# Out projection of a decoder layer as seven half-size products instead of eight, with the gate applied to the outputs

## The chip, the cores and the metric

The kernel runs on one core of one Trainium2 chip. The metric is device time in microseconds; a program on one core has one time per run, and the median of the runs is used. Engines: TensorE (PE) multiplies, VectorE (DVE) and ScalarE (ACT) work on tiles in SBUF and PSUM, GpSimd (POOL) on tiles in SBUF; SyncE (SP) and POOL issue DMAs.

## What is computed

One decoder layer on 512 tokens of width 1024 in float32, and a final norm. The part around the change:

```python
merged = sigmoid(ga) * (out_a @ w_branch_swa) + sigmoid(gd) * (out_d @ w_branch_diff)
x = x + gate1 * (merged @ w_out)                      # out projection
h2 = rmsnorm(x, norm2_g) * (1 + scale2) + shift2
a, g = split(h2 @ w_up, 2)                            # up projection, 2 x 2816 columns
a = causal depthwise conv of width 3 over a, + conv_b
x = x + gate2 * ((gelu(a) * g) @ w_down)              # down projection
return rmsnorm(x, final_g)
```

## The kernel before

Every large product is made of three float32r matmuls: a float32 tile is split into a high part (a cast, on ACT) and a low part (tile minus high part, on DVE), and high x high, high x low and low x high are added up in PSUM. "Cast" and "low" below are these two operations; the function `split` (L118) does both, `split_pair` (L110) also takes the buffers. Weights pass through four raw buffers and three pairs of split buffers (`WB = 3`).

The stages in order: adaLN modulation and input projection; the two attention mixers; gate "d" and the branch merge (L938 to L985, eight column tiles j, one gate product and one branch product each); the **out projection** (L1023 to L1066 and `out_step`, L1245); residual, square sums and norm, the transposes of the normalised tokens (`turn2`) and their modulation (`early`, `mod_one`); the **up projection** in 11 pairs J of column tiles; the down projection with the last residual and norm.

In the merge, tile j is made on DVE in `tdall` (three slots) and split to `mgh[j]`, `mgl[j]` (L970 to L972). The out projection takes the merged columns as the stationary side and rows of `w_out` as the moving side: for k = 0 to 7 a row block of 128x1024 is loaded by SP, multiplied by gate 1 on DVE (L1029) and split. For each of four token blocks t and two column halves three 128x512 matmuls are added into one of eight PSUM banks: 8 x 4 x 2 x 3 = 192. The last three k run token by token, so that tokens 0 and 1 are through early: their residual sum (`add_x`), square sum (`square2`), norm (`norm_a` to `norm_c`; the power -0.5 is made on POOL, L177) and transposes lie beside the matmuls of tokens 2 and 3.

The up projection multiplies, for each pair J, halves of the tokens and halves of the rows in seven products instead of eight: a slot of 24 matmuls of 128x256 each, named p1, m5, m6, p2, m7, p3, p4 (`mul_slot`, L1185). It needs sums of weight blocks (made by accumulating DMAs on POOL's queue, `load_raw`, or by `sum_w` on DVE) and sums of the modulated tokens (`t1n`, `b12`, `b21`, on DVE). What follows a slot (copies, sums, convolution, GELU) is in `behind` and `conv`. The down projection uses the same scheme.

What sets the order: up to the out projection TensorE's order is written out and a scheduler places the other engines' instructions; from the last three k of the out projection to the end of pair 1 of the up projection (`man`, from L1326) all engines run in the order written. Every engine works through its queue in order.

Of the kernel before, what the change touches and what calls it, by code (L numbers as in the profile page):

```python
# [8 lines left out]
F32 = mybir.dt.float32  # L9
F32R = mybir.dt.float32r  # L10
# [4 lines left out]
P = 128  # L15
# [40 lines left out]
def kernel(  # L56
# [877 lines left out]
    def gpart(i, shape, name, dt=F32):  # L934
        return bp.tile(shape, dt, tag=f"gT{i}", name=name)


    mg = [[bp.tile([P, 2, S], F32R, tag="gx", bufs=5, name=f"mg{i}{b}") for b in "hl"] for i in range(2)]  # L938
    mg += [[bp.tile([P, 2, S], F32R, tag="gx", bufs=5, name="mg2h"), bp.tile([P, 2, S], F32R, tag="y", name="mg2l")]]
    mg += [[bp.tile([P, 2, S], F32R, tag="fgb", name="mg3h"), gpart(5, [P, 2, S], "mg3l", F32R)]]  # L940
    mgh, mgl = ([mg[k // 2][b][:, k % 2] for k in range(KT)] for b in range(2))
# [51 lines left out]
    TAIL = 3  # L993
    xnp = [gpart(i, [P, 2, D], f"xn{i}") for i in range(2)]
    g1b = gpart(4, [P, D], "g1b")
    g1bias = xnp[0][:, 0]
    brow(g1b, mod_rows[0])
    brow(g1bias, b_ada[0, 2 * D : 3 * D])
    nc.vector.tensor_add(g1b, g1b, g1bias)
    nc.vector.tensor_scalar_mul(g1b, g1b, 0.5)  # L1000
# [25 lines left out]
    def load_rows(src, k, name, gate):  # L1026
        r = raw_tile([P, D], name)
        nc.sync.dma_start(r, src[k * P : (k + 1) * P, :])
        nc.vector.tensor_mul(r, r, gate)  # L1029
        return split_pair(r, [P, D], name)  # L1030

    def tok_proj(acc, lh, ll, wts, nk, done, half_done=None):
        def step(k, t, hfs=(0, 1)):
            wh, wl = wts[k]
            a = lh(k)[:, t * P : (t + 1) * P]
            b = ll(k)[:, t * P : (t + 1) * P]
            for hf in hfs:
                sl = slice(hf * S, (hf + 1) * S)
                nc.tensor.matmul(acc[t][hf], a, wh[:, sl], start=k == 0, stop=False)
                nc.tensor.matmul(acc[t][hf], a, wl[:, sl], start=False, stop=False)  # L1040
            for hf in hfs:
                sl = slice(hf * S, (hf + 1) * S)
                nc.tensor.matmul(acc[t][hf], b, wh[:, sl], start=False, stop=k == nk - 1)

        for k in range(nk - TAIL):
            for t in range(NT):
                step(k, t)
        for t in range(NT):
            for hfs in ((0,), (1,)) if t == NT - 1 else ((0, 1),):
                for k in range(nk - TAIL, nk):  # L1050
                    step(k, t, hfs)
                if half_done is not None:
                    half_done(t, hfs)
            done(t)


# [3 lines left out]
    oacc = eight("oc")  # L1060
# [4 lines left out]
    wo = [load_rows(wout, k, f"wo{k}", g1b) for k in range(KT)]  # L1065

    def add_and_stat(acc, dst, x, wpool, name):
        ss = []
        for hf in range(2):
            sl = slice(hf * S, (hf + 1) * S)  # L1070
            nc.vector.tensor_add(dst[:, sl], x[:, sl], acc[hf])
            sq = wpool.tile([P, S], F32, tag="sq2", bufs=1, name=f"sq{name}{hf}")
            s1 = wpool.tile([P, 1], F32, tag="ss2", bufs=8, name=f"ss{name}{hf}")
            nc.scalar.activation(sq, dst[:, sl], AF.Square, accum_out=s1)
            if hf == 0:
                nc.vector.tensor_scalar(s1, s1, 1.0 / D, EPS, ALU.mult, ALU.add)
            ss.append(s1)
        rs = wpool.tile([P, 1], F32, tag="rs2", bufs=4, name=f"rs{name}")
        rstd_m2(rs, ss[1], 1, D, wpool, plus=ss[0])
        return rs  # L1080

# [69 lines left out]
    for i, name in enumerate(("p1", "p2")):  # L1151
        first_low = prep(0, name, (early_w[i][:, 0], early_w[i][:, 1]))
        W[1, name] = early_w[2 + i][:, 0], early_w[2 + i][:, 1]
    m5w = gpart(4, [P, 2, 4, 256], "m5w", F32R)
    with tc.issue_after(splits[-3][0].ins), tc.issue_after(splits[-3][1].ins):
        prep(0, "m5", (m5w[:, 0], m5w[:, 1]))
    with tc.issue_after(first_low[1].ins):
        sum_w(0, "m6")
# [86 lines left out]
    def out_step(t, k, hfs=(0, 1)):  # L1245
        wh, wl = wo[k]
        a, b = (m[k][:, t * P : (t + 1) * P] for m in (mgh, mgl))
        for hf in hfs:
            sl = slice(hf * S, (hf + 1) * S)
            nc.tensor.matmul(oacc[t][hf], a, wh[:, sl], start=k == 0, stop=False)  # L1250
            nc.tensor.matmul(oacc[t][hf], a, wl[:, sl], start=False, stop=False)  # L1251
        for hf in hfs:
            sl = slice(hf * S, (hf + 1) * S)
            nc.tensor.matmul(oacc[t][hf], b, wh[:, sl], start=False, stop=k == KT - 1)  # L1254

    ssq, r2, xns = {}, {}, {}

    def add_x(t, hf):
        sl = slice(hf * S, (hf + 1) * S)
        nc.vector.tensor_add(x1[:, t, sl], x1[:, t, sl], oacc[t][hf])  # L1260
# [7 lines left out]
    def norm_a(t):  # L1268
        nc.vector.tensor_scalar(ssq[t, 0], ssq[t, 0], 1.0 / D, EPS, ALU.mult, ALU.add)
        r2[t] = rstd_start(ssq[t, 1], 1, D, bp, plus=ssq[t, 0])  # L1270

    def norm_b(t):
        rs = bp.tile([P, 1], F32, tag="rs2", bufs=4, name=f"rso{t}")
        rstd_end(rs, *r2[t], 1, bp)
        xns[t] = xnp[t // 2][:, t % 2]
        return rs
# [45 lines left out]
    for k in range(KT - TAIL):  # L1322
        for t in range(NT):
            out_step(t, k)
    last = range(KT - TAIL, KT)
# [4 lines left out]
    def hi_early(i):  # L1330
        nc.scalar.copy(W[1, f"p{i}"][0], R[1, f"a1{i}"])

    def lo_early(i, q):
        hi, lo = W[1, f"p{i}"]
        V.tensor_sub(lo[:, q], R[1, f"a1{i}"][:, q], hi[:, q].bitcast(F32))

    hi_early(1)
    lo_early(1, slice(0, 4))
    for k in last:
        out_step(0, k)  # L1340
    add_x(0, 0)
    add_x(0, 1)
    square2(0)
    norm_a(0)
    norm_c(0, norm_b(0))
    hi_early(2)
    for k in last:
        out_step(1, k)
    add_x(1, 0)
    add_x(1, 1)  # L1350
    square2(1)
    lo_early(2, q0)
    norm_a(1)
    lo_early(2, q1)
    norm_c(1, norm_b(1))
    for k in last:
        out_step(2, k)
    add_x(2, 0)
    add_x(2, 1)
    out_step(3, last[0], (0,))  # L1360
    tps = {g: turn2(0, g) for g in (0, 1)}
    for k in last[1:]:
        out_step(3, k, (0,))
    for k in last:
        out_step(3, k, (1,))
    square2(2, (0,))
    early(0, "act")
    square2(2, (1,))
# [3 lines left out]
    early(1, "act")  # L1372
    early(1, "hi")
    norm_a(2)
    early(0, "lo")
    add_x(3, 0)
    early(1, "lo")
    square2(3, (0,))
    add_x(3, 1)
    square2(3, (1,))  # L1380
    for g in (2, 3):
        tps[g] = turn2(0, g)
    mul_slot(0, "p1")
    early(2, "vec")
    norm_a(3)
    early(3, "vec")
    for g in (2, 3):
        early(g, "act")
        early(g, "hi")
# [4 lines left out]
    mul_slot(1, "p1", (0,))  # L1394
# [18 lines left out]
    mul_slot(0, "p2", (0,))  # L1413
# [6 lines left out]
    mul_slot(0, "p2", (1,))  # L1420
    mul_slot(1, "p1", (1,))
# [10 lines left out]
    low_w(0, "m6")  # L1432
    lo_t(0, t1n, q0)
# [10 lines left out]
    sum_w(0, "p3")  # L1444
# [5 lines left out]
    V.tensor_sub(b12, b22, b12)  # L1450
    cast_w(0, "m7")
    hi_t(2, b12)
    V.scalar_tensor_tensor(b21, t1n, -1.0, b21, ALU.mult, ALU.subtract)
    hi_t(3, b21)
    behind(0, "m6")
    low_w(0, "m7")
    lo_t(2, b12)
    cast_w(1, "m5")
    mul_slot(0, "m7")
    lo_t(3, b21)  # L1460
    low_w(1, "m5")
    behind(0, "p3")
    mul_slot(1, "m5")
    behind(1, "p1")
    cast_w(0, "p4")
    sum_w(1, "m6")
# [3 lines left out]
    cast_w(1, "m6")  # L1470
    behind(0, "p2")
    conv_bias(0, 0)
    low_w(1, "m6")
    behind(1, "m5")
    mul_slot(1, "m6")
    sum_w(1, "p3")
# [388 lines left out]
```

## Time and profile before

| what | value |
|---|---|
| median of 3 runs | 696.21 us (696.03 to 697.71) |
| span of the profiled execution (it has no other time) | 696.6 us |
| out projection with its transposes | 314.66 to 360.96 us of the span |
| busy in 314.6 to 360.0: PE, DVE, ACT, POOL | 45.0, 26.6, 17.2, 3.8 us of 45.4 |
| busy in 374.0 to 412.0: PE, DVE, ACT, POOL | 38.0, 37.8, 26.1, 5.1 us of 38.0 |
| granted TensorE clock | 0.999 of full |

Times in the profile count from the start of the span. A group's row gives line, engine, operation, output<-inputs, shape, count, busy time, mean length in ns and idle time ahead of it. A timeline row gives start, length, engine, line, operation. A row of the chain that ended last gives start, length and what held the chain. Consecutive matmuls overlap, so their rate is read from starts, not lengths.

### The profile page before, as it was taken

The numbers are of one execution on the slowest core, as the hardware profiler recorded it, in microseconds if no ns is written. First come the engines' busy times: TensorE is split into PE (matmuls) and PEld (weight loads), VectorE is DVE, ScalarE is ACT, GpSimd is POOL, SyncE is SP. The second block draws the span as 40 slices with busy tenths as digits, with TensorE's granted clock in tenths as the row PEclk, the third lists the DMA queues.
The fourth block names the chain that finished last, engine by engine and source line by source line (L and its number), as shares of the span: only waits on it lengthen the run. The fifth ranks groups of instructions, "written<-read, shape, count | busy, mean of one in ns | idle before, by whom it ended". The sixth has DMA issues, their size and how long they took to land.

```text
span 696.6 us, 11353 instructions
## 1 busy us (share of the span) xinstructions
PE 685.0 (98%) x4247; PEld 598.4 (86%) x4247; DVE 573.3 (82%) x1093; ACT 377.9 (54%) x673; POOL 82.8 (12%) x100
## 2 busy tenths in 40 slices
PE   8999999999999999999999999999999999999995
PEld 8877877777787888888789999999999999888885
DVE  5999987888885557663679998888888999979997
ACT  5655675544552333331468756555555666655665
POOL 3000000000101000000020111111111102540300
PEclk9999999999999999999999999999999999999999
DMA  9985454454435676229817688786879738997903
GB/s 311 326 251 166 143 173 129 135 161 124 124 100 154 197 220 206 93 97 280 275 45 146 151 193 197 164 209 188 207 214 220 172 127 222 184 204 202 166 1 120
DMA packets 115862, 121.81 MB, mean 175 GB/s; under 512 B 4383, under 2 KB 93280, under 8 KB 115808
## 3 DMA queue, kind: packets, MB, share of 16 engines
q1 hardware_dynamic: 96894, 95.09, 43.0%
q0 software_dynamic: 18720, 25.73, 21.9%
q8 instruction: 33, 0.54, 0.3%
q10 hardware_dynamic: 194, 0.28, 0.1%
q14 instruction: 21, 0.17, 0.1%
HBM read 118.97 MB, written 2.11 MB: 174 GB/s over the span
## 4 chain that ended last, share of the span: by engine, by line
PE 64%; DMA 2%; DVE 1%; ACT 1%; issue 0%; POOLq 0%; DVEq 0%; ACTq 0%
PE up L1194 32%; PE dc L1809 15%; PE pgd L123 2%; PE pgd L125 2%; PE pgd L124 2%; DMA wo<-in_w_out_dram 2%; PE pB L125 1%; PE pB L123 1%; PE pB L124 1%; PE oc L1251 1%; PE oc L1254 1%; PE oc L1250 1%; PE pga L123 1%; PE pga L125 1%; PE pga L124 1%; DMA wa<-in_w_up_dram 1%
## 5 line engine op out<-in xcount | busy, mean ns | idle before, releaser
L1194 PE MATMUL up<-t,m_whi 128*128 128x256 f32 x512 | 93.1, 283 | 0.0
L1194 PEld LDWEIGHTS up<-t,m_whi 128*128 128x128 f32 x512 | 79.9, 192 | 0.0
L1194 PE MATMUL up<-t,m_wlo 128*128 128x256 f32 x256 | 72.5, 283 | 0.0
L1194 PE MATMUL up<-bh,p_whi 128*128 128x256 f32 x232 | 65.8, 283 | 0.0
L1194 PE MATMUL up<-bl,p_whi 128*128 128x256 f32 x232 | 65.7, 283 | 0.0
L1194 PE MATMUL up<-bh,p_wlo 128*128 128x256 f32 x232 | 65.7, 283 | 0.0
L810 DVE SCALAR_TENSOR_TENSOR arow<-ra,cs,arow 128x512 f32<-128x512 f32 x56 | 42.0, 750 | 23.1 <-DMA ra<-in_w_ada_dram 22.6
L1194 PEld LDWEIGHTS up<-t,m_wlo 128*128 128x128 f32 x256 | 49.2, 192 | 0.0
L1194 PEld LDWEIGHTS up<-bl,p_whi 128*128 128x128 f32 x232 | 44.6, 192 | 0.0
L1194 PEld LDWEIGHTS up<-bh,p_whi 128*128 128x128 f32 x232 | 44.6, 192 | 0.0
L1194 PEld LDWEIGHTS up<-bh,p_wlo 128*128 128x128 f32 x232 | 44.6, 192 | 0.0
L1103 POOL DMA_DIRECT2D s<-in_w_up_dram x21 | 27.0, 1360 | 141.0 <-DMA s<-in_w_up_dram 62.5
L1131 ACT CAST m_whi<-s 128x1024 fp32r<-128x1024 f32 x31 | 32.5, 1047 | 11.1 <-DVE s L1125 7.7
L1135 DVE TENSOR_TENSOR m_wlo<-s,m_whi 128x1024 fp32r<-128x1024 f32 x31 | 37.8, 1219 | 0.0
L1194 PE MATMUL up<-t,p_whi 128*128 128x256 f32 x176 | 32.2, 283 | 0.0
L177 POOL TENSOR_TENSOR r<-ms,mhalf 128x1 f32<-128x1 f32 (+1 forms) x16 | 13.1, 822 | 132.4 <-DVE ms L175 73.6
L829 POOL DMA_DIRECT2D mod_rows<-row x8 | 5.1, 642 | 194.2 <-ACT row L828 194.2
L724 ACT ACTIVATE sd<-sd,dmx 128x128 f32<-128x128 f32 (+3 forms) x32 | 17.7, 556 | 19.2 <-DVE dmx L716 19.2
L1194 PEld LDWEIGHTS up<-t,p_whi 128*128 128x128 f32 x176 | 27.5, 192 | 0.0
L1201 ACT ACTIVATE gT<-a,cv 128x512 f32<-128x512 f32 x22 | 17.7, 813 | 16.9 <-DVE a L1236 15.8
L1131 ACT CAST p_whi<-wa 128x1024 fp32r<-128x1024 f32 x18 | 18.7, 1041 | 12.6 <-PE up L1194 9.0
L1135 DVE TENSOR_TENSOR p_wlo<-wa,p_whi 128x1024 fp32r<-128x1024 f32 x18 | 22.0, 1223 | 3.8 <-ACT p_whi L1131 3.8
(479 smaller groups left out, 2085.7 us busy)
## 6 DMA issues: line engine op xcount, KB each, us to landing
ra<-in_w_ada_dram SPq DMA_DIRECT2D x32, 512.0 KB, 3.9
wa<-in_w_up_dram SPq DMA_DIRECT2D x22, 512.0 KB, 4.2
s<-in_w_up_dram SPq DMA_DIRECT2D x21, 512.0 KB, 4.8
s<-in_w_up_dram POOLq DMA_DIRECT2D x21, 512.0 KB, 6.4
adaw<-in_w_ada_dram SPq DMA_DIRECT2D x16, 512.0 KB, 5.3
w<-in_w_in_dram SPq DMA_DIRECT2D x12, 512.0 KB, 4.4
a<-in_w_up_dram SPq DMA_DIRECT2D x11, 512.0 KB, 4.7
b<-in_w_down_dram SPq DMA_DIRECT2D x10, 512.0 KB, 4.3
```

Of the source, the lines that this page charges most:

```text
L123: nc.tensor.matmul(o, lh, rh, start=start, stop=False)
L124: nc.tensor.matmul(o, lh, rl, start=False, stop=False)
L125: nc.tensor.matmul(o, ll, rh, start=False, stop=stop)
L177: nc.gpsimd.tensor_tensor(r0, ms, mhalf[:, :n], ALU.pow)
L724: exp = nc.scalar.activation(pm[m], pm[m], AF.Exp, bias=mx[:, m : m + 1], scale=slope, accum_out=lsum[:, m : m + 1])
L810: nc.vector.scalar_tensor_tensor(ac, r[:, a], cc, ac, ALU.mult, ALU.add)
L1103: nc.gpsimd.dma_start(dst, upblock(*blk), accum_op=ALU.add)
L1131: nc.scalar.copy(W[J, name][0], R[J, SRC[name]])
L1135: nc.vector.tensor_sub(lo, R[J, SRC[name]], hi.bitcast(F32))
L1194: nc.tensor.matmul(o[u], w[:, k, cu], b[:, k], start=name in ("p1", "m5", "p2") and k == 0 and x == 0, stop=k == 3 and x == 2, skip_group_ ...
L1201: nc.scalar.activation(grow(j), av[J][:, u], AF.Identity, bias=cv[:, 66 + j : 67 + j], scale=cv[:, 44 + j : 45 + j])
L1809: nc.tensor.matmul(bank2[u][:, sl], a[:, q, cu], b[:, q, sl], start=first_mm and x == 0, stop=last_mm and x == 2, skip_group_check=name no ...
```

## The change

The out projection is written as seven products of halves: tokens in halves (0 to 255, 256 to 511), inner rows as even and odd tiles of 128, columns in halves of 512. Each product is 4 inner tiles x 2 token blocks x 3 matmuls of 128x512. It needs sums of merged halves (`out_sums`: four sums of 128x256 per pair of column tiles on DVE, each split) and sums of blocks of `w_out`, made by accumulating DMAs on POOL's queue behind the low of the block's earlier form. Gate 1 no longer multiplies the weights; it multiplies the outputs (`post` on DVE, `minus_gated` on POOL, `gate_nlo`), and is itself loaded in two halves with its bias added by DMA. `norm_a` may take the halves' square sums in either order.

Then the hand-written order up to pair 1 is made anew: weights of p1, p2 and m5 of pair 0 are split within the out projection; p1 and p2 of pairs 0 and 1 run undivided; three lows of 128x1024 (p4's first, m5's and the second p2), the sums for m6 and p3 of both pairs and one sum of modulated tokens move to POOL. In all, POOL gets eight elementwise operations of 128x512 and eight of 128x1024; its queue gets eight loads of 512 KB from `w_out`, and SP's has six instead of eight. The tiles of `w_up` that follow take buffers which the out projection's merged tiles held.

```diff
-    mgh, mgl = ([mg[k // 2][b][:, k % 2] for k in range(KT)] for b in range(2))
+    SH = S // 2
+    NQ = KT // 2
+    od1 = [bp.tile([P, 2, S], F32R, tag="gx", bufs=5, name=f"od1_{q}") for q in range(NQ)]
+    ev = [bp.tile([P, NQ, SH], F32R, tag=g, name=f"ev{b}") for g, b in (("y", "h"), ("fgb", "l"))]
...
-            split(mgh[j], mgl[j], td)
+            q, odd = divmod(j, 2)
+            if odd:
+                split(od1[q][:, 0], od1[q][:, 1], td)
+                out_sums(q, tds[j - 1], td)
+            else:
+                split(ev[0][:, q], ev[1][:, q], td[:, :SH])
...
+    def out_sums(q, a, b):
+        lo, hi = slice(0, SH), slice(SH, S)
+        d, s2, s3, s4 = (sraw[:, i] for i in range(4))
+        nc.vector.tensor_sub(d, b[:, hi], a[:, hi])
+        nc.vector.scalar_tensor_tensor(s2, d, -1.0, a[:, lo], ALU.mult, ALU.subtract)
+        nc.vector.scalar_tensor_tensor(s4, s2, -1.0, b[:, lo], ALU.mult, ALU.subtract)
+        nc.vector.tensor_sub(s3, a[:, lo], a[:, hi])
+        for name, raw in (("d", d), ("s4", s4), ("s2", s2), ("s3", s3)):
+            split(sm[name][:, 0, q], sm[name][:, 1, q], raw)
...
-        nc.vector.tensor_mul(r, r, gate)
-        return split_pair(r, [P, D], name)
...
+    opass = dict(
+        m1=(oU, och, (0, 1)), p2=(oX, ostr, None), m5=(oV, och, (1, 1)), p3=(oV, osec, (0, 1)),
+        m6=(oU, och, (1, 0)), m7=(oU, osec, None), p4=(oU, och, None),
+    )
...
+    def oprep(name, g, on_pool=False):
+        _, src, add = opass[name]
+        wh = wp.tile([P, 2, S], F32R, tag="whi", bufs=WB, name=f"o{name}h{g}")
+        wl = wp.tile([P, 2, S], F32R, tag="wlo", bufs=WB, name=f"o{name}l{g}")
+        if on_pool:
+            nc.scalar.copy(wh, src[g])
+            nc.gpsimd.tensor_tensor(wl, src[g], wh.bitcast(F32), ALU.subtract)
+        else:
+            split(wh, wl, src[g])
+        if add is not None:
+            nc.gpsimd.dma_start(src[g], oblock(g, *add), accum_op=ALU.add)
+        ow[name, g] = wh, wl
...
+    def omul(name, gs=(0, 1), us=(0, 1)):
+        o = opass[name][0]
+        for g in gs:
+            wh, wl = ow[name, g]
+            for u in us:
+                for i in range(2):
+                    q = 2 * g + i
+                    ah, al = oside(name, q, u)
+                    for x, (a, b) in enumerate(((ah, wh), (ah, wl), (al, wh))):
+                        nc.tensor.matmul(
...
+    def post(u, acc, gate, add, first):
+        if first is not None:
+            V.tensor_add(acc[:, u], acc[:, u], first[u])
+        V.tensor_mul(acc[:, u], acc[:, u], gate)
+        d = x1h(u, add)
+        (V.tensor_sub if add else V.tensor_add)(d, d, acc[:, u])
...
+    def pool_gate(u, acc):
+        nc.gpsimd.tensor_tensor(acc[:, u], acc[:, u], g1b[1], ALU.mult)
+    def pool_sub(u, acc):
+        nc.gpsimd.tensor_tensor(x1h(2 + u, 1), x1h(2 + u, 1), acc[:, u], ALU.subtract)
+    def sum_pool(J, name):
+        src = R[J, SRC[name]]
+        nc.gpsimd.tensor_tensor(src, src, R[J, "a11" if name == "m6" else "a12"], ALU.add)
+    def lo_pool(J, name):
+        hi, lo = W[J, name]
+        nc.gpsimd.tensor_tensor(lo, R[J, SRC[name]], hi.bitcast(F32), ALU.subtract)
...
+    omul("m6")
+    V.tensor_add(ocv[:, 0], ocv[:, 0], oU[0])
+    oprep("m7", 1)
+    V.tensor_add(ocv[:, 1], ocv[:, 1], oU[1])
+    oprep("p4", 0, True)
+    hi_early(1, "p1")
+    post(0, ocv, g1b[1], 1, None)
+    square2(0, (1,))
+    post(1, ocv, g1b[1], 1, None)
+    oprep("p4", 1)
+    omul("m7")
+    square2(1, (1,))
+    nc.scalar.copy(ocv[:, 0], oU[0])
     norm_a(0)
+    nc.scalar.copy(ocv[:, 1], oU[1])
+    norm_a(1)
+    norm_halves(0, norm_b(0))
+    norm_halves(1, norm_b(1))
+    minus_gated(0, ocv)
+    minus_gated(1, ocv)
...
+    omul("p4", us=(0,))
     tps = {g: turn2(0, g) for g in (0, 1)}
+    omul("p4", us=(1,))
...
+    lo_pool(0, "m5")
     for g in (2, 3):
         tps[g] = turn2(0, g)
     mul_slot(0, "p1")
+    mul_slot(1, "p1")
...
     norm_halves(2, norm_b(2))
     norm_halves(3, norm_b(3))
     early(2, "lo")
     early(3, "lo")
-    mul_slot(1, "p1", (0,))
+    hi_early(1, "p2")
+    sum_pool(0, "m6")
+    lo_pool(1, "p2")
...
     low_w(0, "m6")
+    sum_pool(0, "p3")
...
     mul_slot(0, "m6")
-    sum_w(0, "p3")
     cast_w(0, "p3")
...
-    V.tensor_sub(b12, b22, b12)
+    nc.gpsimd.tensor_tensor(b12, b22, b12, ALU.subtract)
...
-    sum_w(1, "m6")
...
+    sum_pool(1, "m6")
...
+    sum_pool(1, "p3")
```

More of the change, by code (lines that the diff above doesn't have):

```diff
@@ L1059, with oblock @@
     braw = {}
-    oacc = eight("oc")
+    oU, oX, oV = (
+        [fbank("oc0"), fbank("oc1")], [sbank("oc2"), vbank("oc3")], [sbank("oc4"), sbank("oc5")],
+    )
+    wo4 = wout.rearrange("(q a p) n -> p q a n", a=2, p=P)
+    def oblock(g, a, hf):
+        return wo4[:, 2 * g : 2 * g + 2, a, hf * S : (hf + 1) * S]
+    ochain = gpart(4, [P, NQ, S], "ochain")
+    och = [ochain[:, 2 * g : 2 * g + 2] for g in range(2)]
+    for g in range(2):
+        nc.sync.dma_start(och[g], oblock(g, 0, 0))
@@ L1061 @@
+    for name, g in (("m1", 0), ("m1", 1), ("p2", 0)):
+        oprep(name, g)
     wa1 = gpart(2, [P, 2, 4, 256], "wa1")
@@ L1350, with hi_early @@
-    add_x(1, 1)
-    square2(1)
-    lo_early(2, q0)
-    norm_a(1)
[L1354 to L1360, printed above, removed]
-    tps = {g: turn2(0, g) for g in (0, 1)}
[L1362 to L1366, printed above, removed]
+    both = range(2)
+    def hi_early(J, name):
+        nc.scalar.copy(W[J, name][0], R[J, SRC[name]])
@@ L1383 @@
     mul_slot(0, "p1")
+    mul_slot(1, "p1")
+    add_nlo(1)
+    norm_a(2, 1)
+    early(2, "act")
+    square2(3, (0,))
     early(2, "vec")
-    norm_a(3)
+    early(3, "act")
+    norm_a(3, 1)
     early(3, "vec")
-    for g in (2, 3):
-        early(g, "act")
-        early(g, "hi")
+    early(2, "hi")
+    early(3, "hi")
     norm_halves(2, norm_b(2))
```

214 lines of the change are left out of this document (102 added, 112 removed).

## Prediction

> **What bounds the kernel now.** I read the head of the page first, then the chain that ended last, the waits of TensorE, and the busy time by stage.
>
> ```profile
> span 696.6 us, 11353 instructions
> PE 685.0 (98%) x4247; PEld 598.4 (86%) x4247; DVE 573.3 (82%) x1093; ACT 377.9 (54%) x673; POOL 82.8 (12%) x100
> ```
> ```profile
> PE pc L168 <- DMA crow<-in_c_dram: 2.4, 1, 2.4
> PE pga L123 <- ACT ta L840: 1.1, 1, 1.1
> PE oc L1251 <- DVE wo_l L120: 0.4, 1, 0.4
> PE td L742 <- DVE dls L727: 0.3, 1, 0.3
> PE pss L765 <- DVE qkv L465: 0.2, 1, 0.2
> ```
> ```profile
> 314.60:360.00 45.40, 45.02 (x202) 36.88 (x202) 26.58 (x44) 17.21 (x27) 3.82 (x4) 1.00 0.67 210
> 360.00:374.00 14.00, 14.00 (x121) 14.00 (x120) 12.80 (x27) 12.20 (x24) 4.49 (x4) 1.00 0.79 144
> 374.00:412.00 38.00, 38.00 (x319) 38.00 (x318) 37.79 (x53) 26.13 (x41) 5.11 (x4) 1.00 0.65 147
> ```
> In the stage rows the figures after the length are busy time of PE, weight loads, DVE, ACT and POOL, then granted clock, DMA share and GB/s. TensorE is busy 98% of the span and its five waits add up to 4.4 us. So a matmul that goes is time that goes, if nothing else comes late. The out projection (first row) has slack on DVE (26.6 of 45.4 us). The up projection behind it has none: DVE is busy 37.8 of 38.0 us, and TensorE doesn't wait. That is where this change can lose what it wins.
>
> **The change part by part.** *Matmuls.* Rates come from the chain in order of time (start, length):
>
> ```profile
> 314.66 0.43 PE oc L1250
> 347.75 0.45 PE oc L1254 x2
> 353.19 0.45 PE oc L1254 x2
> 360.09 0.88 PE th L1289 x8
> ```
> Between the second and third row stand four steps of six 128x512 matmuls: 24 in 5.44 us. Before, the stage runs 192 of them; after, 7 products x 4 row blocks x 2 token blocks x 3 = 168. The 24 that go are worth **-5.44 us**. From 314.66 to 360.09 are 45.43 us; 192 matmuls take 43.52 and the first eight transposes 0.88, so 1.03 us is waiting. The chain there runs through the last weight's DMA, cast and low; with the eight gated rows of w_out that wait goes: **-1.03 us**. What is late next is worked out below. A product now lasts 5.44 us; starting at 314.66 as before, p2, m5, p3, m6, m7 and p4 start at 320.1, 325.5, 331.0, 336.4, 341.9 and 347.3, and p4 with its transposes ends at 353.6.
>
> *Work ahead of the stage.* Each pair of merged column tiles gets four sums and four more lows of 128x256. From the rows below (0.42 us a 128x256, 0.69 a 128x512) a pair goes from 1.38 to 4.47 us on DVE, +12.4 us for four. Six of the eight gate products (1.22 us each) stood in this stage and go: net +5.1 us. ACT gets 16 more 128x256 casts. The stage is
>
> ```profile
> 262.00:314.40 52.40, 52.40 (x243) 42.32 (x241) 36.62 (x43) 17.21 (x24) 1.10 (x2) 1.00 0.41 133
> L1232 DVE TENSOR_TENSOR a<-a,up 128x256 f32<-128x256 f32 x4 | 1.5, 418 | 0.0
> L1260 DVE TENSOR_TENSOR x<-x,oc 128x512 f32<-128x512 f32 x8 | 5.2, 682 | 1.3 <-PE oc L1254 1.3
> L1135 DVE TENSOR_TENSOR m_wlo<-s,m_whi 128x1024 fp32r<-128x1024 f32 x7 | 8.5, 1220 | 0.0
> L1131 ACT CAST m_whi<-s 128x1024 fp32r<-128x1024 f32 x7 | 7.3, 1050 | 5.0 <-DVE s L1125 5.0
> ```
> DVE goes to about 42 of 52.4 us, beside gate matmuls: nothing on the path. Without that cover it would be 5 us. m1 needs only the even columns, ready one gate earlier; p2, the first to need the last odd column, has 5.4 us.
>
> *Weights.* Fourteen casts and lows replace eight: a product needs 2 x 1.05 us on ACT and 2 x 1.22 on DVE in 5.44 us. That fits. With three buffers a cast waits until the matmuls of the weight three places earlier are through, which is one product (5.44 us) ahead of its own use; cast and low one after the other take 2.27.
>
> *Accumulating loads.* The sums of w_out blocks are made by eight 512 KB loads on POOL's queue, each behind the low that still reads the old block, and behind the s1 load for the up projection, which waits there for its base.
>
> ```profile
> s<-in_w_up_dram POOLq DMA_DIRECT2D x21, 512.0 KB, 6.4
> ```
> ```profile
> s_t<-in_w_up_dram POOLq DMA_DIRECT2D x1, 512.0 KB, 12.2
> ```
> The median landing is 6.4 us over the run, 12.2 for the one issued in this stage. m5's first weight is split at 320.1 + 1.05 + 1.22 = 322.4; its block lands at 328.8 to 334.6, and m6's low is done at 331.1 to 336.9, needed at 336.4. That low can't be earlier than 333.3 (buffer free at 331.0). p4's block then lands at 339.7 to 349.1, and with cast and POOL's low (below) is ready at 341.8 to 352.0, needed at 347.3. So this chain costs 0 to 4.7 us. (On POOL the gate product of m5's result waits for ACT's copy, 0.9 us after 331.0, and p4's loads are queued behind it; they wait for m6's low longer than that.) SP's next w_up loads now wait for tiles that the product p4 still reads, so fewer transfers compete late in the stage; I stay near the lower end and take **+0.6 us**. Those delayed loads (s3 and s1 of the first pairs) go out at about 354 and are first needed at m7 of pair 0, near 377: covered by 23 us; with 12.2 us each and their second loads behind three POOL operations they would still land by then.
>
> *Outputs and norm.* Tokens 0 and 1 are complete after m6, at 341.9 (its first half 1.36 us earlier, at 340.5). Then on DVE in order: add 0.69, m7's low 1.22, add 0.69, four of 0.69, p4's low 1.22: 6.6 us. Rows of the norm follow: two pairs of small ones, two powers on POOL at 0.55, ends and halves (0.57 each), some 3 us. That ends at 350.1 from the earlier start and 351.5 from the later; the transposes between the halves of p4 want it at 350.0. So 0 to 1.5 us; I take **+0.7**. Queued behind it are the lows of the first modulated tiles, due 3.6 us later behind p4's second half.
>
> *POOL's arithmetic.* Eight 128x512 and eight 128x1024 operations with two inputs, of a kind that the trace doesn't have. Nearest rows:
>
> ```profile
> L153 POOL TENSOR_SCALAR_AFFINE_SELECT ddf<-ddf 128x512 f32<-128x512 f32 x1 | 0.6, 605 | 0.0
> L150 POOL TENSOR_SCALAR_AFFINE_SELECT dsw<-dsw 128x256 f32<-128x256 f32 x1 | 0.4, 391 | 0.0
> ```
> One input costs 0.214 us per 256 and 0.177 fixed. So 128x1024 takes 1.03 us if a second input is free, 1.89 if it is read after the first; 0.61 and 1.03 for 128x512. I take the upper, because nothing in the trace shows POOL reading two at once: 8 x 1.03 + 8 x 1.89 = 23.4 us on an engine busy 3.8 of 45.4 us. Its results are due late enough: p4's low is bounded above, after p4 come transposes (0.88) and p1 of both pairs (5.76), so the next transposes stand at 360.3, m6 of pair 0 at 370.8 and p3 at 373.6; their sums are due 2.3 us ahead, at 368.5 and 371.3. The Trainium skill, GPSIMD Engine Reference, section 3.1, measures 4497 ns for 2048 columns, an estimate of 2.25 us for 1024; by it POOL would have 27 us of work. No row here shows such an operation.
>
> *The up projection anew.* p1 and p2 of both pairs follow each other undivided; the matmuls are the same. The stretch from the transposes of tokens 2 and 3 to m5 shrinks:
>
> ```profile
> 365.27 0.87 PE th L1289 x8
> ```
> ```profile
> 374.02 3.04 PE L1194 MATMUL up<-t,m5w 128*128 128x256 f32 x24
> 376.90 0.40 PE L1194 MATMUL up<-t,m_whi 128*128 128x256 f32 x2
> ```
> It was 8.75 us and becomes two transposes of 0.88 and two products of 2.88: 7.5. DVE's lead there falls by 1.2 us. Four 128x1024 operations leave DVE in the dense stretch, 4 x 1.13 = 4.5 us by the spacing of
>
> ```profile
> 376.92 1.22 DVE L1450 TENSOR_TENSOR braw<-braw 128x1024 f32<-128x1024 f32 x1
> 378.05 1.22 DVE L1453 SCALAR_TENSOR_TENSOR braw<-s_t,braw 128x1024 f32<-128x1024 f32 x1
> 406.76 1.22 DVE L1135 TENSOR_TENSOR m_wlo<-s,m_whi 128x1024 fp32r<-128x1024 f32 x1
> 408.58 0.40 PE L1194 MATMUL up<-t,m_whi 128*128 128x256 f32 x2
> ```
> The last pair is where DVE's lead is least: the low ends at 407.98, its product starts at 408.58, 0.6 us. With 4.5 - 1.2 us more it is 3.9: no wait, if POOL leaves DVE alone. I cost it at **0**.
>
> **Sum.** 696.6 - 5.44 - 1.03 + 0.6 + 0.7 = 691.4 us of span. The profiled execution has no time beside its span; it lies 0.4 above the median 696.21 of the runs (696.03 to 697.71). So the forecast is **691.0 us**.
>
> **Rivals.** *POOL holds up DVE (slower).*
>
> ```profile
> 353.43 0.94 POOL L177 TENSOR_TENSOR r<-ms,mhalf 128x1 f32<-128x1 f32 x1 [3.67 <-DVE ms L175]
> 362.39 0.55 POOL L177 TENSOR_TENSOR r<-ms,mhalf 128x1 f32<-128x1 f32 x1 [2.55 <-DVE ms L175]
> ```
> ```profile
> 353.27 0.68 DVE L1335 TENSOR_TENSOR early<-wa,early 128x512 fp32r<-128x512 f32 x1
> 362.61 0.21 DVE L183 SCALAR_TENSOR_TENSOR rt<-r,ms 128x1 f32<-128x1 f32 x1
> ```
> The same power takes 0.55 us alone and 0.94 when it is issued while DVE reads two SBUF tiles: POOL waits for DVE. Whether DVE waits for POOL as long, no row tells; the small operation at 362.61 inside the power kept its usual 0.2 us, which speaks against. If it does: (a) p4's low on POOL, 1.89 us, stands before the norm, which has no slack; (b) behind the second power POOL has the sum for m6 and p2's low, 3.78 us, before DVE may end norm and lows of tokens 2 and 3. Behind the powers of tokens 0 and 1 (done at about 349.5) four gate operations (1.03 each), m5's low (1.89) and two powers end at 356.6, half a us later where the squares come last, ends and halves 1.5 later: 358.5, 1.8 ahead of 360.3. Costs 2.0; (c) the four moved operations hold DVE 7.6 us where they spared it 4.5; with the shorter lead 7.6 - 4.5 + 1.2 - 0.6 = 3.7 us. Together 7.6: **698.6 us**. It turns slower once POOL holds DVE for two thirds of that. The Trainium skill, SBUF — State Buffer, section "Who interferes with whom", has this rule: a VectorE instruction with two SBUF inputs and a GpSimd instruction that reads SBUF exclude each other, and whichever started first keeps the other out to its end. The trace agrees in one direction (0.94 against 0.55).
>
> *The sums of w_out land late.* The 4.7 us of that chain instead of 0.6: **695.1 us**. For it: 12.2 us in this stage, and a DMA share of 0.67 there with half a dozen more software loads; against it: SP's loads that wait.
>
> That the products aren't fewer is excluded: 168 matmuls are in the program's order.
>
> **How the numbers follow.** Forecast 0.50, POOL against DVE 0.28, late sums 0.14, other lateness of the seven products' preparation that costs more than the 6.5 us won 0.08. No new wait gives 696.2 - 6.5 = 689.7, the lower end; the upper reaches past the first rival to 699.5, leaving out part of it and the last case. A measurement here tells 0.3% (2.1 us) from no change: faster is the forecast and a third of the late sums, 0.54; same is the rest of these and the mild part of POOL's case, 0.16; slower 0.30.
>
> **What would show it.** After: 168 oc matmuls at 5.44 us a product; no TensorE wait over 1 us between m1 and m5 of pair 0; POOL's 128x1024 at 1 to 1.9 us while DVE's stay at 1.22. POOL's case shows as DVE groups grown beyond 1.22 and waits of up on lows; late sums as ACT casts of m6 or p4 waiting for ochain. I am wrong if the first matmul of m1 starts later than 314.7, or if a product waits for a buffer.

## The result, and the profile after

The changed kernel takes **717.04 us** (median of 4 runs, 715.9 to 718.14) against 696.23 beside it: ratio 1.0295, 95% interval 1.0278 to 1.0312. The forecast was 691.0 with a range to 699.5. The profiled execution took 717.19 us, with a span of 715.4.

The head of the page after, with the rows of busy tenths for TensorE, its granted clock and the DMAs, and the chain that ended last:

```profile
span 715.4 us, 11408 instructions
PE 688.2 (96%) x4223; PEld 599.0 (84%) x4223; DVE 597.8 (84%) x1122; ACT 393.7 (55%) x705; POOL 124.0 (17%) x126
PE   8999999999999999998876999999999999999995
PEclk9999999999999999999988999999999999999998
DMA  9976445444455664669737399878779738997902
PE 79%; DVE 11%; DMA 4%; issue 3%; ACT 1%; POOL 1%; SPq 0%; POOLq 0%; DVEq 0%; ACTq 0%
```

TensorE has 24 matmuls fewer (4223 for 4247), as the change says, yet it is busy 3 us longer, and in two slices in the middle its granted clock falls. In the slices around 330 to 390 us it isn't full any more. The waits of TensorE say for what:

```profile
PE up L1226 <- DVE t L1339: 4.3, 1, 4.3
PE th L1308 <- DVE xn L1301: 4.2, 3, 3.6
PE oc L1113 <- DVE om6l L120: 2.3, 1, 2.3
PE oc L1113 <- ACT oc_fgb L1365: 1.9, 1, 1.9
PE oc L1113 <- ACT oc_v L1428: 1.8, 1, 1.8
PE pB L125 <- DVE wbd L120: 1.3, 1, 1.3
```

The first five of these lie between the start of m1 (314.50) and the end of m5 of pair 0, the last in the merge. From m1 to p3 of pair 0 both kernels do the same products, but for the 24 matmuls, and this stretch holds most of the result. The busy time by stretch, before and after (columns: length, then busy time of PE, weight loads, DVE, ACT, POOL, granted clock, DMA share, GB/s):

```profile
314.66:379.79 65.13, 64.75 (x369) 56.61 (x370) 45.11 (x74) 33.68 (x57) 8.31 (x8) 1.00 0.67 186
```
```profile
314.50:397.93 83.43, 68.10 (x346) 57.99 (x346) 69.95 (x89) 45.62 (x78) 40.51 (x28) 0.90 0.73 177
330.00:350.00 20.00, 15.81 (x61) 12.08 (x61) 16.86 (x16) 11.33 (x17) 10.75 (x9) 0.91 1.10 227
```

It is 18.3 us longer (83.43 for 65.13), where the forecast had 5.2 less. Behind it the kernels run alike: 317.5 us remain after, 316.8 before. Ahead of it, in the merge, there is a smaller loss; the rows of 300 to 310 before and after, and what DVE stood still for:

```profile
300.00:310.00 10.00, 10.00 (x45) 8.26 (x44) 6.06 (x7) 4.38 (x6) 0.00 (x0) 1.00 0.30 105
```
```profile
300.00:310.00 10.00, 8.67 (x39) 6.85 (x38) 5.51 (x10) 3.28 (x6) 2.09 (x2) 1.00 0.51 84
304.98 0.43 DVE L1026 TENSOR_SCALAR g1b<-g1b 128x512 f32<-128x512 f32 x1 [4.39 <-DMA g1b<-in_b_ada_dram]
```

DVE waits 4.39 us for the second half of gate 1 with its bias, the low of a branch weight behind it comes late, and TensorE waits 1.3 us (`pB <- DVE wbd`). From the first branch product to the out projection are 57.5 us, 55.9 before.

In the stretch from m1 on DVE shows 69.95 us of busy time instead of 45.11, POOL 40.51 instead of 8.31, and in 330 to 350 the DMA engines are full (share 1.10) at only 227 GB/s. What DVE's busy time is made of shows in the timeline, on DVE and then on POOL (start, length):

```profile
373.57 2.43 DVE L183 SCALAR_TENSOR_TENSOR rt<-r,ms 128x1 f32<-128x1 f32 x1
376.64 0.21 DVE L183 SCALAR_TENSOR_TENSOR rt<-r,ms 128x1 f32<-128x1 f32 x1
383.45 6.86 DVE L1339 TENSOR_TENSOR t<-s_t,t 128x512 fp32r<-128x512 f32 x2
391.60 1.29 DVE L1339 TENSOR_TENSOR t<-s_t,t 128x512 fp32r<-128x512 f32 x2
```
```profile
373.58 2.41 POOL L1379 TENSOR_TENSOR s_t<-s_t,wa 128x1024 f32<-128x1024 f32 x1
383.61 3.85 POOL L1379 TENSOR_TENSOR s_t<-s_t,wa 128x1024 f32<-128x1024 f32 x1
386.35 3.40 POOL L1530 TENSOR_TENSOR braw<-braw 128x1024 f32<-128x1024 f32 x1
```

The first operation of DVE works on one column, usually takes 0.21 us, and lasts 2.43: until POOL's operation of 2.41 us, started beside it, is over (375.99 and 376.00). The two lows at 383.45 usually take 1.29 us together. They last 6.86, across two of POOL's operations that follow each other (the second ends at 389.75); this is the wait of 4.3 us inside m5. So two theories stand: **POOL's two-input operations keep DVE out** (the prediction's first rival, dearer than it was priced), and **blocks of w_out land late** (the second). A third is that DVE simply has too much to do, whoever works beside it; a fourth, that the falling clock costs the time.

### The profile page after: what moved, and what is told of

Its sections match the earlier page's. It is cut to its first block, busy times and chain, and to the rows that moved or that the text cites. A ratio compares the mean times of both kernels' runs of the same rounds, so it can differ in the third digit from the quotient of the medians.

```text
span 715.4 us, 11408 instructions
## 1 busy us (share of the span) xinstructions
PE 688.2 (96%) x4223; PEld 599.0 (84%) x4223; DVE 597.8 (84%) x1122; ACT 393.7 (55%) x705; POOL 124.0 (17%) x126
## 4 chain that ended last, share of the span: by engine, by line
PE 79%; DVE 11%; DMA 4%; issue 3%; ACT 1%; POOL 1%; SPq 0%; POOLq 0%; DVEq 0%; ACTq 0%
PE up L1226 30%; PE dc L1889 15%; PE a L360 4%; PE pga L123 2%; PE pga L125 2%; PE pga L124 2%; PE oc L1113 1%; DMA osec<-in_w_out_dram 1%; PE pgd L123 1%; PE pgd L124 1%; PE pgd L125 1%; PE pw L123 1%; PE pk L123 1%; DMA ra<-in_w_ada_dram 1%; PE pw L124 1%
```

## The experiments

Names for short: "all on DVE" is the changed kernel with POOL's sixteen operations on DVE; osec0 is the block of w_out for p3 and m7.

**POOL's operations given back to DVE, all and in part.**

```diff
-        nc.gpsimd.tensor_tensor(acc[:, u], acc[:, u], g1b[1], ALU.mult)
+        nc.vector.tensor_tensor(acc[:, u], acc[:, u], g1b[1], ALU.mult)
```
The same edit in all six places for the first run; in the four of the out projection and the early weights (eleven operations) for the second; in `sum_pool` and at `b12` (five operations) for the third. (The expectations speak of twelve operations, and of three or four sums; the edits move eleven, and four sums with one subtraction.)

> All sixteen of POOL's operations with two inputs go back to VectorE, at the same places in the order; nothing else changes. Theory 1 (a POOL operation that reads two SBUF tiles and a VectorE operation on SBUF tiles keep each other out, and TensorE's clock falls after the waits that follow): the waits at the transposes between the halves of p4 (4.4 us in the changed kernel), at m5 of pair 0 (6.2 with its slow matmuls) and the slow matmuls behind them go, 12 to 18 us of 717.0: 699 to 705 us, granted clock back over 0.9 in 355 to 395 us. Rival (VectorE has simply too much work in these stages, whoever else works): eight operations of 0.69 and eight of 1.13 us, 14.6 us of work, are put on top of it: 717 to 728 us.

> Only the twelve POOL operations of the out projection's stage and of the first up products (four gate products, four subtractions, the lows of p4, of m5 and of p2 on pair 1... those that belong to the outputs and to early weights) go back to VectorE; the three sums and the subtraction of the dense stretch stay on POOL. Theory 1: the wait at the transposes and the slow second half of p4 go, 6 to 10 us; the wait before m5 of pair 0 stays at 3 us or more: 707 to 711 us. Rival (too much work on VectorE): 717 to 723 us.

> Only the three or four sums for the up projection's weights and one subtraction of 128x1024 go back to VectorE; the out stage keeps its POOL operations. Theory 1: the wait inside m5 of pair 0 (4.6 us) with its slow matmuls (about 2.5 us) goes, the waits between p4's halves stay: 709 to 712 us. Rival (too much work on VectorE): 717 to 722 us.

Measured: **706.95** (706.61 to 707.74), 712.21 and 711.23 us. The parts give 4.8 and 5.8 us, together 10.6; all at once 10.1. That is below the range that the first theory gave the first two runs (12 to 18, 6 to 10), and clearly against the third theory: 14.6 us more work on DVE made the kernel faster. The long wait at m5 (`up <- t`) is gone in all three runs; in the second the stretch of m5 shrank to 4.4 us too, against its expectation. The wait at the transposes between p4's halves (`th <- xn`) is down to 0.4 us in the first and the second run and stays in the third. In the second the sum that POOL kept, 2.37 us from 369.94, holds DVE's `rt` of one column (2.38 from 369.95), and the next transposes wait 2.7 us for it:

```profile
PE oc L1113 <- ACT oc_fgb L1365: 2.5, 1, 2.5
PE oc L1113 <- ACT oc_v L1428: 2.5, 1, 2.5
PE up L1226 <- DVE t L1339: 1.0, 2, 0.6
```
```profile
PE oc L1113 <- ACT oc_fgb L1365: 4.5, 1, 4.5
PE th L1308 <- DVE rt L183: 2.7, 1, 2.7
```
```profile
PE th L1308 <- DVE xn L1301: 3.6, 1, 3.6
PE oc L1113 <- ACT oc_fgb L1365: 2.4, 1, 2.4
PE up L1226 <- DVE t L1339: 1.0, 2, 0.5
```
(All on DVE; the second run; the third.) With all on DVE 10.6 us over the kernel before remain, and the longest waits are now those of out products.

**The mechanism by itself**, in the kernel before, which has none of the change. Four operations of 128x1024 on POOL in the dense stretch, each reading something that DVE has just made, writing a tile that is free. One of the four in the first run is shown; the second run has `tensor_scalar` of `bl[:, 2]` (times 2, plus 1) in its place, the third the same on one column and then a `memset` of 128x1024.

```diff
     V.tensor_sub(bl[:, 2], b22, bh[:, 2].bitcast(F32))
+    nc.gpsimd.tensor_tensor(gT[5][:, 0:2].rearrange("p a s -> p (a s)"), x1[:, 0], bl[:, 2].rearrange("p a n -> p (a n)").bitcast(F32), ALU.mult)
     behind(0, "m5")
     low_w(0, "p3")
...
```

> The kernel before, with four more multiplications of 128x1024 on POOL in the dense stretch of the up projection; each reads two tiles of SBUF that are long done, and nothing reads what they write. Each starts when a VectorE low is done, apart from the others. Theory 1 (POOL and VectorE exclude each other): VectorE loses 2.4 us to each, 9.6 in all, less the 0.6 to 2 us that it is ahead there: 703 to 706 us. If a POOL operation leaves VectorE alone: 696 us, VectorE's 128x1024 operations at 1.22 us throughout.

> The kernel before with four more operations of 128x1024 on POOL at the same places as in the run that gave 703.69 us, but with one input (times two plus one) instead of two. If what excludes VectorE is that POOL reads SBUF at all: as long as POOL's operation lasts, about half of the 7.4 us or more: 699 to 704 us. If it takes two POOL inputs: 696 us.

> The kernel before with four fills of 128x1024 on POOL at the same places, each behind a 128x1 operation of POOL's that reads the low just made: POOL only writes. If POOL's reading is what excludes VectorE: 695.5 to 697 us, VectorE's 128x1024 operations at 1.22 us beside the fills. If any POOL work on SBUF does: 699 us or more.

Measured: **703.69** us with two inputs (+7.4, interval of the ratio 1.009 to 1.012), **698.57** with one (+2.0, 1.0019 to 1.0038; its range began at 699), **696.54** with fills (0.9986 to 1.0007: nothing). The first one's timeline, DVE and POOL:

```profile
371.11 1.22 DVE L1125 TENSOR_TENSOR s_t<-s_t,wa 128x1024 f32<-128x1024 f32 x1
372.25 3.43 DVE L1447 TENSOR_TENSOR bl<-braw,bh 128x1024 fp32r<-128x1024 f32 x1
375.60 1.21 DVE L1135 TENSOR_TENSOR p_wlo<-s_t,p_whi 128x1024 fp32r<-128x1024 f32 x1
376.73 3.42 DVE L1452 TENSOR_TENSOR braw<-braw 128x1024 f32<-128x1024 f32 x1
```
```profile
371.33 3.26 POOL L1443 TENSOR_TENSOR gT<-x,t 128x1024 f32<-128x1024 f32 x1 [6.23 <-DVE t L1320]
375.81 3.26 POOL L1448 TENSOR_TENSOR gT<-x,bl 128x1024 f32<-128x1024 f32 x1 [1.21 <-DVE bl L1447]
```

So each engine keeps the other out; below this is called the lock, and it goes both ways. POOL is issued at 371.33, waits until DVE's operation ends (372.33, 1.0 us), and then runs some 2.3; DVE's next lasts until POOL is through (374.59) plus its own 1.1. The first three cost DVE 2.2 us each, the last 1.5. Beside the fills DVE keeps its length, and beside one input it loses less, because POOL is done sooner:

```profile
375.06 0.96 POOL L1450 MEMSET gT<- 128x1024 f32 x1
```
```profile
374.87 1.22 DVE L1454 TENSOR_TENSOR braw<-braw 128x1024 f32<-128x1024 f32 x1
```
```profile
375.41 1.89 POOL L1448 TENSOR_SCALAR gT<-bl 128x1024 f32<-128x1024 f32 x1 [1.23 <-DVE bl L1447]
```
```profile
376.31 2.05 DVE L1452 TENSOR_TENSOR braw<-braw 128x1024 f32<-128x1024 f32 x1
```
(Fills: POOL, DVE; one input: POOL, DVE.) So it is POOL's reading of SBUF that excludes a DVE operation with two SBUF inputs, as the Trainium skill has it (SBUF — State Buffer, section "Who interferes with whom": not a GpSimd instruction that only writes). The trace agrees with that rule in each of the three runs.

**The late block osec0, alone and with all on DVE.**

```diff
-    nc.sync.dma_start(osec[0], oblock(0, 1, 1))
+    with tc.high_priority(offset=HP):
+        nc.sync.dma_start(osec[0], oblock(0, 1, 1))
```

> Only the place of one load changes: the block of w_out for p3 and m7 (osec0) is issued on SP's queue ahead of the loads of x instead of behind them. Theory 2 (blocks of w_out land late: osec0 lands at 329.5 us, and p3 waits 2.1 us for it): p3 starts 2 us earlier, and what waits behind it in m6 shrinks too: 712 to 715 us. Theory 1 alone (TensorE waits for VectorE behind POOL later on anyway, so an earlier p3 is lost again before the transposes): 716.5 to 717.5 us.

> Both changes together: all sixteen of POOL's two-input operations on VectorE and the block for p3 and m7 (osec0) loaded ahead of x. With VectorE alone the run took 706.95 us, and its VectorE and ScalarE stood still for 5.5 and 5.9 us before the first cast for p3, waiting for osec0; everything behind in their fixed order (the lows of m6, m7 and p4) was late by that. Theory (the late block holds the whole order of the stage, not only p3): the 9.3 us that the stage still loses mostly go: 697 to 700 us. Rival (the stage's transfers are too many: DMA share 1.1 in 330 to 345, so some block lands late in whatever order): 703 to 706 us.

Measured: 715.95 us (713.85 to 716.56), not to be told from 717.0, and **707.06**, as without it (706.95). p3 does start without a wait, at 331.43 and 331.87, but the time comes back as longer stretches of m6 and m7 (9.42 and 8.44 us with all on DVE, instead of 5.44). The second run lies a little above the range of its rival (703 to 706) and far from the theory's: that some block is late whatever the order is the nearer reading.

**The accumulating loads**, with all on DVE and osec0 early: left out; plain loads in their place (shown); accumulating, but with `[:, :, :32]` on both sides, 32 of 512 columns.

```diff
         if add is not None:
-            nc.gpsimd.dma_start(src[g], oblock(g, *add), accum_op=ALU.add)
+            nc.gpsimd.dma_start(src[g], oblock(g, *add))
```

> As the run before it (VectorE for all, osec0 early), but the eight accumulating loads of w_out are left out, so that m5, p3's successors m6, m7 and p4 multiply by blocks that aren't the sums; nothing waits for those eight loads and 4 MB less are moved in the stage. If the transfers are what is left, the seven products run undisturbed: 691 to 696 us, and 4 us or more below the run before it. If the order of the VectorE work is what is left: within 1.5 us of the run before it.

> All arithmetic on VectorE and osec0 early (707.06 us), with the eight accumulating loads as plain loads of the same blocks into the same tiles from the same queue: same bytes, same waits for the lows, no addition (so the blocks aren't the sums). In the trace 4.03 MB of accumulating loads take 42.9% of the DMA engines where 6.29 MB of plain ones take 37.7%: 2.9 against 1.6 us of all sixteen engines per 512 KB. If this is the price: 700 to 703 us. If the bytes as such or the wait for the low are the price: 705 to 707 us.

> As the run before it, but the loads accumulate, each only the first 32 of 512 columns (the rest of the sums is left out): same waits and issues, a sixteenth of the bytes. If transfer time is the price of these loads: 698.5 to 700.5 us, as without them. If it is their issue and their wait for the low that still reads the old block: 704 us or more.

Measured: **698.98**, **699.89** and **699.52** us, for 707.06 with the full accumulating loads. The first gained more than the 4 us that blame the transfers but missed their 691 to 696; the second is just below its range for the price of adding, the third inside its range for transfer time. So the price is neither the issue nor the wait for the low, nor the bytes, but the adding, which takes more time of the DMA engines. Some 1.5 of the 8.1 us are won back ahead of m1: without these loads, or with plain ones, the merge takes 55.9 us again. The queue rows in 310 to 362 us (packets, MB, share of the 16 engines), with accumulating and with plain loads, and the busy rows of 330 to 350, in the same order:

```profile
q0 software_dynamic: 2408, 4.15, 44.4%
```
```profile
q0 software_dynamic: 1392, 3.67, 21.9%
```
```profile
330.00:350.00 20.00, 16.57 (x66) 12.20 (x66) 14.11 (x18) 9.39 (x15) 4.01 (x4) 0.95 1.12 227
```
```profile
330.00:350.00 20.00, 19.08 (x85) 15.24 (x84) 18.48 (x31) 13.14 (x23) 3.13 (x5) 1.00 0.55 200
```
44.4% of 52 us for 4.15 MB are 5.6 us per MB, 21.9% for 3.67 MB are 3.1: an accumulating 512 KB block takes 2.9 us of all sixteen engines. The second row still holds one accumulating load (of s1, for the up projection); without it a plain block takes 1.4. With the accumulating loads the engines are full for 20 us (1.12), the blocks of `ochain` land after 10.8 us (median) instead of 6.5, and DVE stands still for 6 of the 20.

**The same in the changed kernel, with POOL's operations kept**: no accumulating loads; and no accumulating loads with osec0 early (the edits above).

> The changed kernel with its sixteen operations on POOL, but without the eight accumulating loads of w_out (the products after p2 multiply by blocks that aren't the sums). Without these loads the version with all arithmetic on VectorE took 8.1 us less (707.06 to 698.98). If the two losses are separate, the same comes off here: 708 to 710 us. If late blocks only fill time in which POOL holds VectorE up anyway: 713 us or more.

> The changed kernel, POOL's sixteen operations kept, with both transfer losses taken away: osec0 loaded ahead of x, no accumulating loads. The run without accumulating loads alone gave 716.28 us, but there p3 still waited 3.6 us for osec0. If the losses are separate and osec0 hid the gain: 716.3 - 3.6 or lower, 706 to 712 us (a loss to POOL alone of 7 to 13 us over the 698.98 of the same kernel with VectorE). If VectorE, held up by POOL, sets the time on its own: 713 to 716.5 us, a loss to POOL alone of 14 to 17 us.

Measured: 716.28 (713.81 to 717.23) and **709.90** us. Each repair of a late block alone gave about 1 us (so the first run fits its second reading, late blocks in time that is lost anyway), and both 7.1. Without the loads p3 still waited for osec0 (3.5 us by the waits), with osec0 early the accumulating blocks were late. What POOL costs by itself, against the same work on DVE, is 709.90 - 698.98 = **10.9 us**, within the range of "the losses are separate".

**What is left.** All on DVE, osec0 early, no accumulating loads, and thirteen of DVE's operations left out:

```diff
     def pool_gate(u, acc):
-        nc.vector.tensor_tensor(acc[:, u], acc[:, u], g1b[1], ALU.mult)
+        return
```
and the same in `pool_sub`, `sum_pool` and at `b12`.

> All arithmetic on VectorE, osec0 early, no accumulating loads (698.98 us), and thirteen operations left out altogether: the gate products and subtractions of the m5 and p4 results (eight of 128x512), the four sums for m6 and p3 of pairs 0 and 1 and one subtraction of 128x1024: 11.2 us less work on VectorE. If VectorE, busy 59.3 of the 64.5 us from m1 to p3 of pair 0, is what still keeps the time from 689.7, most of it goes: 690 to 693 us. If something else does (the transposes, buffers, TensorE's order): 697 us or more.

Measured: **693.99** us (ratio 0.9945 to 0.9973), outside both ranges, nearer to the first. The stretch from m1 to p3 of pair 0, without and with the thirteen:

```profile
314.71:376.08 61.37, 59.80 (x345) 52.18 (x345) 52.99 (x91) 45.33 (x77) 7.58 (x8) 1.00 0.69 187
```
```profile
312.75:377.26 64.51, 60.96 (x345) 52.12 (x345) 59.31 (x100) 44.29 (x76) 7.56 (x8) 1.00 0.65 178
```
With them DVE is busy 59.3 of 64.5 us, 14.2 more than before. So the third theory holds a part after all: with all on DVE, these thirteen operations cost 5.0 us. 3.1 of them lie in this stretch; behind it 319.6 us remain with them and 317.2 without. Still 4.3 us lie above 689.7. In the stretch they show as one wait of p4, `PE oc <- ACT oc_v`, 1.0 us (the stretch of m7 is 6.66 instead of 5.44: p4 adds into the banks that ACT still copies), one of 0.5 at the transposes and shorter ones; these were not tried by themselves.

**The clock.** 36 matmuls that nothing uses, ahead of m5 of pair 0.

```diff
+    for _ in range(36):
+        nc.tensor.matmul(psum(0, "m5")[0], W[0, "p2"][0][:, 0, 0:P], bh[:, 1, 0], start=True, stop=True, skip_group_check=True)
     mul_slot(0, "m5")
```

> The changed kernel with 36 more 128x256 matmuls just ahead of m5 of pair 0, whose results are overwritten by m5 and used by nothing; at 0.12 us each they take 4.3 us, the length of the wait (4.57 us) inside m5. If the clock falls because TensorE stands still (granted clock 0.69 in 390 to 400 us, matmuls at 0.21 instead of 0.12 us after the wait), m5 and m6 of pair 0 run at 0.12 us: 2 to 2.5 us faster than the changed kernel, 714.5 to 715 us, granted clock above 0.95 there. If the slow matmuls have another reason: 717 to 718 us.

Measured: 716.62 us (715.84 to 717.75), between the two ranges: no gain. The changed kernel, then the filled one:

```profile
385.00:390.00 5.00, 1.07 (x9) 0.86 (x8) 5.00 (x1) 0.00 (x0) 4.75 (x3) 0.94 1.22 193
390.00:395.00 5.00, 4.64 (x21) 4.64 (x22) 4.12 (x7) 4.06 (x8) 0.00 (x0) 0.50 0.84 187
```
```profile
385.00:390.00 5.00, 5.00 (x44) 5.00 (x44) 5.00 (x1) 0.40 (x1) 5.00 (x3) 1.00 1.19 186
390.00:395.00 5.00, 4.92 (x41) 4.69 (x40) 4.12 (x6) 3.30 (x6) 0.45 (x1) 1.00 1.05 225
```
The granted clock did stay at 1.00 instead of 0.50, and m5 and m6 ran at full rate. But DVE (4.12 us busy in both) was no further, and the next two m products took 7.1 us instead of 5.76. The fall of the clock is real, and its cause here is the standing still, since matmuls that nothing uses prevent it; at this place it cost nothing. The two other places where matmuls ran at half rate (from 341.3 and from 364.3) were not tried, so the fourth theory is settled for m5 alone.

## Why the prediction was wrong

| step | forecast | what the runs showed |
|---|---|---|
| 24 fewer matmuls | -5.44 us | right: 168, a product 5.44 us wherever nothing waits |
| the wait for the last weight goes | -1.03 | it goes; p4's wait for ACT's copies of its banks takes its place (1.0 in the freest run, 1.8 in the changed kernel) |
| sums ahead of the stage | 0 | m1 starts at 314.50 (314.7 was the bound), but the merge took 1.7 more |
| accumulating loads and late blocks | +0.6 (0 to 4.7) | 7.1 with POOL's operations, 8.1 without for the loads alone |
| norm against transposes | +0.7 | not tried alone; with all on DVE the wait is 0.4 |
| POOL's arithmetic, as long as it leaves DVE alone | 0 | 10.9 against the same work on DVE, 15.9 against leaving thirteen of the sixteen out |
| up projection anew | 0 | not separable: part of the 10.9 and of the 5.0 of DVE's own work |

**The step that failed first** is "no wait, if POOL leaves DVE alone", costed at 0. POOL doesn't leave it alone. The mechanism was the first rival, and its place was right: the norm and transposes of tokens 0 to 3 and the moved operations in the dense stretch. The evidence against it could not bear the weight: the small operation that kept 0.2 us (`rt<-r,ms` at 362.61) did run beside a power on POOL, but that power reads a single column. The changed kernel shows the same again,

```profile
356.21 1.10 POOL L177 TENSOR_TENSOR r<-ms,mhalf 128x1 f32<-128x1 f32 x2 [3.83 <-DVE sso L1286]
```
```profile
356.82 0.22 DVE L183 SCALAR_TENSOR_TENSOR rt<-r,ms 128x1 f32<-128x1 f32 x1 [0.36 <-POOL r L177]
```
and 2.43 us for the same operation beside 1024 columns. So a power tells nothing of the long operations; why it doesn't hold DVE is not shown. The size of this rival failed too: 7.6 us for 10.9; and the 0 stood for work that takes nothing from DVE, for which the nearest run is the one without thirteen of the operations, 15.9 us below (709.90 - 693.99). A 128x1024 operation takes 2.41 us, not 1.89. The estimate of 2.25 from the Trainium skill (GPSIMD Engine Reference, section 3.1) was the nearer one. And one of POOL's behind another, at 383.61 and 386.35, left DVE no turn between them, which the price had not allowed for. The remark that the case turns slower at two thirds of its price is wrong too: there it reaches only 696.1; by the prediction's own 2.1 us it needs 7.3 of the 7.6.

**The second step that failed** is the +0.6 for the accumulating loads. I priced the landing of `ochain`'s blocks at 6.4 to 12.2 us from medians of the kernel before, and argued that "fewer transfers compete late in the stage". The opposite is measured: share 1.10 in 330 to 350. The term left out is the DMA engines' time: 1.5 us more per accumulated block, eight blocks. It shows less in `ochain`, which lands after 9.1 us (median; 10.8 with all on DVE and osec0 early), than in the blocks of `osec` for m7, which the sum doesn't follow: in that version they land after 13.2 us, and ACT's casts, in their fixed order, wait 3.8 us for them and 2.8 for those of m6 and p4. osec0 was not in the sum at all: it is issued behind four loads of x on SP's queue at 319.7, its cast starts at 329.6, and behind the casts on ACT stand the copies of m5's banks (`oc_fgb`, 1.9 us) for which p3, due at 331.0, waits.

**The term for the work ahead of the stage, "nothing on the path", failed as well**, and only luck hid it. It counted DVE's work but not what DVE waits for: gate 1's second half is loaded on the queue that also has the first accumulating block of w_out (issued at 294.40). The merge took 57.5 us for 55.9, and without accumulating loads it takes 55.9. That m1 still starts on time is chance: the stages ahead, which the change leaves alone, ended at 257.0 here and at 258.7 in the profile before, and anywhere from 256.9 to 258.9 in the other profiles. The span of 696.6, too, belongs to an execution about 2 us longer than the median, since in every other profile the time is some 2 us above the span; the prediction took it for 0.4. This didn't move the forecast, as 696.2 less the 5.2 of its terms gives the same 691.0.

**The last error is in how the cases were put together.** The two rivals had chances of 0.28 and 0.14 as if one excluded the other. Both happened: 7.6 + 4.7 - 0.6 on top of 691.0 would have been 702.7, above the range's upper end, and 708 with the two sizes measured. The other 9 us are DVE's own work (5.0) and the short waits that are left, which no case held. The thing that ties them may be DVE: its work between 314 and 400 us has grown from 45.1 to 59.3 us (counted with POOL's part), so that a lock or a late block finds little time to hide in. This fits the runs (one late block repaired gives 1 us, both 7) but was not tried by itself. The prediction looked at DVE's lead only at the last pair. The chain of the versions:

| version | us |
|---|---|
| changed kernel | 717.04 |
| osec0 early, no accumulating loads | 709.90 |
| and POOL's sixteen operations on DVE | 698.98 |
| and thirteen of these operations left out | 693.99 |
| forecast with no new wait | 689.7 |

None of the versions that compute everything is below the kernel before; the best is all on DVE, 706.95 us.

## What to carry to other kernels

POOL is no second VectorE for arithmetic on SBUF: as long as it reads SBUF, a DVE operation with two SBUF inputs stands still, for 2.4 us per 128x1024 that would cost DVE 1.13 itself; give POOL fills, or work in time that DVE has free. Price an accumulating load by the time it takes of the DMA engines (here twice a plain one), beside all that is in flight in that stage, and look for the block that stands behind others on its queue. When two losses delay the same engine, repair both before judging either: one alone gave 1 us, both 7.

## What the runs showed of the hardware

- The lock reaches DVE operations of one column with two inputs (2.43 us for 0.21) and the norm's scaling of 128x512 by a column (1.57 for 0.48); two that read PSUM took 0.99 us together beside a POOL operation from 362.97 to 366.18, as they do beside none:

```profile
357.27 1.57 DVE L1301 TENSOR_SCALAR xn<-x,rso 128x512 f32<-128x512 f32 x1
364.41 0.99 DVE L1316 TENSOR_SCALAR braw<-th,c 128x256 f32<-128x256 f32 x2 [0.46 <-ACT braw L1318]
```
```profile
357.29 1.28 POOL L1372 TENSOR_TENSOR oc_v<-oc_v,g1b 128x512 f32<-128x512 f32 x1
362.97 3.21 POOL L1383 TENSOR_TENSOR m5wl<-s_t,m5wh 128x1024 fp32r<-128x1024 f32 x1 [0.44 <-ACT m5wh L1347]
```

- TensorE's clock halves after some waits: behind the 4.57 us ahead of m5's later matmuls these follow each other every 0.21 us instead of 0.12 for 5.9 us, and behind a wait of 2.65 us at 338.66 the 128x512 matmuls took 0.43 instead of 0.23 for 3.7 us. Behind gaps of 2.32 us ahead of p3 (333.05) and 2.16 ahead of p4 (355.76) they kept 0.23. The Trainium skill (TensorE: Matmul & The Clock Gate, Part 1) speaks of an idle window of some 3.4 us; the wait at 338.66 was shorter and the clock fell all the same.
